# Spreading the conditioning rows over two branches, and moving merge additions and four early low parts from GpSimd to VectorE

## The chip, the core and the metric

The kernel runs on one core of a Trainium2 chip. The metric is the device time of one execution in microseconds (us). Three executions of the kernel before took 1597.98, 1598.51 and 1600.79 us (median 1598.51).

## The reference

Two layers of a hybrid backbone act on 256 latent tokens and 256 context tokens of width 1024. Both layers share this form; layer 1 needs only the latent output.

```python
sh1, sc1, g1, sh2, sc2, g2 = split(silu(c) @ w_ada[l] + b_ada[l], 6)      # conditioning: 6*1024 numbers, for c and for c_ctx
h = rms_norm(x, norm1[l]) * (1 + sc1) + sh1                               # latent; the same for the context
u_f, dn_qkv, dn_z, dn_ab, da_q, da_k, da_v, gates = split_columns(h @ w_in)
y_f  = fourier_mix(u_f) @ w_f                                             # branch F
q, k, v = silu(centred_depthwise_conv(dn_qkv))                            # 5 taps
y_dn = deltanet_output(bidirectional_deltanet(q, k, v, ...), dn_z) @ w_dn # branch D
y_da = diff_output(differential_attention(...)) @ w_da                    # branch A
g_f, g_dn, g_da = split(sigmoid(gates), 3)
y = (g_f * y_f + g_dn * y_dn + g_da * y_da) @ w_o
x = x + g1 * y
h2 = rms_norm(x, norm2[l]) * (1 + sc2) + sh2
x = x + g2 * (relu(h2 @ w_mlp1)**2 @ w_mlp2)
```

All inputs are fp32. After layer 1 a last RMSNorm gives the output.

## The kernel before

**Matmuls.** Features lie on the 128 partitions, tokens on the free axis (512 in layer 0, 256 for latent-only products). Each fp32 operand is split into a high part (rounded to fp32r) and a low part (the rest), and each product is three fp32r matmuls: high by high, low weight by high, high weight by low (`mm3`). Weights come in tiles `raw` of 128x1024 (512 KB), loaded by SyncE's DMA queue (SP) into a ring of four buffers (`raw_tile`, L238). ScalarE writes the high part `whi` (L254), and the engine `eng`, by default VectorE, writes the low part `wlo = raw - whi` (L255). Layer 1's convolution weights alternate between GpSimd and VectorE, by `turn_dn` in `load_w`. One gate chunk takes 24 matmuls, one half projection chunk 12.

**Conditioning rows.** `Rows` computes adaLN numbers as dot products on VectorE: a row tile of `w_ada` (128x1024, also in the ring `raw`) is multiplied with the silu of `c` and of `c_ctx`, with accumulation: two VectorE instructions into `junk` for one row (L336). The 24 rows 16 to 39 of layer 0 are worked off in its branches D and A: after each of the eight steps of a branch `side()` pops a number from the list `TAKE` and takes so many rows.

**Branches.** `branch(cg, cp, Y, put, side, ahead)` works through eight output chunks j: it opens the gate of a chunk `ahead` steps early (`open_gate`: 24 matmuls into a PSUM bank `pg`, then tanh on ScalarE into `gt`), multiplies Y by the projection chunk (12 matmuls into `pg`), gates the product on VectorE (`gt`, L894), and hands it to `put`. For branch F `put` spills it to DRAM; for D and A it adds it to the tile `merged` (L1148), in D on GpSimd (G), in A on VectorE (V). There are two banks `pg`, and four buffers `gt`. Branch D has three gates opened ahead (`EARLY`), so that its last three steps have no gate of their own.

**Convolution of the DeltaNet.** `dn_pair(0)` computes q, k and v of two heads: product, four multiply-adds on VectorE (`cy`, L632), tanh, `q` or `cy` (L637), then TensorE transposes them (L166). Between its products it opens four early gates of branch F; their low parts are written by GpSimd. In layer 0 the gates 0 and 1 have been produced before by `front0`, so that only gates 2 and 3 load weights there; in layer 1 all four do.

**Order.** Program order gives priorities. A scheduler that works with its own model of durations places the instructions of each engine from these; in chains such as the DeltaNet's they are given by due times (`weave`). Each engine then works through its own list in that order, and a wait holds up all that stands behind it on that engine.

Of the kernel before, what the change touches and what calls it, by code (L numbers as in the profile page):

```python
# [16 lines left out]
ALU = mybir.AluOpType  # L17
# [22 lines left out]

EARLY = 3

TAKE = [2] * 11 + [1, 1, 0, 0, 0]


NP = 3
# [8 lines left out]
C_DN, C_U, C_DA, C_Z, C_GF, C_PF, C_GA, C_PA, C_GD, C_PD, C_WO, C_M1, C_M2 = (  # L55
    0, 12, 16, 28, 32, 40, 44, 52, 56, 64, 68, 76, 108)
# [69 lines left out]
def bcast(ap, n):  # L126
    return ap.unsqueeze(2).broadcast_to([ap.shape[0], ap.shape[1], n])
# [54 lines left out]
def body(tc, A, dbg=None):  # L182
    nc = tc.nc
    weave = Weave(tc)
    V, S, G, PE = nc.vector, nc.scalar, nc.gpsimd, weave
# [47 lines left out]
    def cbank():  # L233
        return bank("pc")
# [141 lines left out]
    def rsqrt_small(x, pool, nm, bufs=2):  # L376

        w = x.shape[1]
        y, e, p_ = (pool.tile([P, 16], F32, tag=nm + c, name=nm + c, bufs=bufs)[:, :w] for c in "yep")
        S.activation(y, x.bitcast(I32), AF.Exp, scale=-0.5 * LN2 / 2 ** 23, bias=rbias)  # L380
        V.tensor_tensor(out=e, in0=y, in1=y, op=ALU.mult)
        V.tensor_tensor(out=e, in0=e, in1=x, op=ALU.mult)
        V.tensor_scalar(out=e, in0=e, scalar1=-1.0, scalar2=1.0, op0=ALU.mult, op1=ALU.add)
        V.tensor_scalar(out=p_, in0=e, scalar1=0.31282382, scalar2=0.37521049, op0=ALU.mult, op1=ALU.add)
        V.tensor_tensor(out=p_, in0=p_, in1=e, op=ALU.mult)
        V.scalar_tensor_tensor(out=p_, in0=p_, scalar=0.5, in1=e, op0=ALU.add, op1=ALU.mult)
        V.scalar_tensor_tensor(out=y, in0=p_, scalar=1.0, in1=y, op0=ALU.add, op1=ALU.mult)
        return y
# [18 lines left out]
    def square_sums(src, acc, pool, tag="sj"):  # L407

        for i in range(src.shape[1]):
            j = pool.tile([P, P], F16, tag=tag, name=tag)  # L410
            S.activation(j, src[:, i], AF.Square, accum_out=acc[:, i:i + 1])
# [54 lines left out]
    def mixer(l, last, front):  # L466
# [101 lines left out]
        def dn_pair(p):  # L568

            q2 = dp.tile([P, 2, n], F32, tag="q2", name="q2")  # L570
            k2 = dp.tile([P, 2, T], F32, tag="k2", name="k2")
            ktm = dp.tile([P, 4, 2, P], F32, tag="ktm", name="ktm")
            vtm = dp.tile([P, 4, 2, P], F32, tag="vtm", name="vtm")
            due, now, started = [], [0.0], []

            def flush(t, least=-1):

                while due and (due[0][0] <= t or min(x_[1] for x_ in due) <= least):
                    now[0], i, fn = due.pop(0)
                    with weave.chain() as at:  # L580
                        at(now[0])
                        fn()

            def later(dt, fn):
                due.append((weave.time + dt, len(started), fn))
                due.sort(key=lambda x_: x_[0])

            def finish(hh_, h, kind, m, dst):
                pt = cbank()
                for t in range(m // P):  # L590
                    PE.transpose(pt[:, t * P:(t + 1) * P], dst[:, t * P:(t + 1) * P], ident)
                pt3 = pt.rearrange("p (t c) -> p t c", c=P)[:, :m // P]
                if kind == 0:
                    square_sums(pt3, ssq[:, h], mp)
                elif kind == 1:
                    ssk = mp.tile([P, 4], F32, tag="ssk", name="ssk", bufs=2)
                    square_sums(pt3, ssk, mp)
                    V.tensor_scalar(out=ssk, in0=ssk, scalar1=EPS, scalar2=None, op0=ALU.add)
                    rk = rsqrt_small(ssk, mp, "rk")
                    V.tensor_tensor(out=ktm[:, :, hh_], in0=pt3, in1=bcast(rk, P), op=ALU.mult)  # L600
                    due.append((now[0] + POST[1], math.inf, partial(back, hh_)))
                    due.sort(key=lambda x_: x_[0])
                else:
                    S.copy(vtm[:, :, hh_], pt3)

            def back(hh_):
                pb = cbank()
                for t in range(4):
                    PE.transpose(pb[:, t * P:(t + 1) * P], ktm[:, t, hh_], ident)
                S.copy(k2[:, hh_], pb)  # L610

            for hh_ in range(2):
                h = 2 * p + hh_
                for kind in range(3):
                    f = 4 * kind + h
                    m = n if kind == 0 else T
                    ps = product(("dn", h, kind), C_DN + f, m)
                    ns = m // L
                    if p == 0 and hh_ == 1 and kind < 2:
                        for i in (2 * kind, 2 * kind + 1):  # L620
                            early[C_GF, i] = open_gate(C_GF, i, G)
                    u = dp.tile([P, 2, L + 4], F32, tag="R", name="cu", bufs=1 + last)
                    G.memset(u[:, :, 0:2], 0.0)
                    G.memset(u[:, :, L + 2:L + 4], 0.0)
                    S.copy(u[:, 0:ns, 2:L + 2], ps[:, :m].rearrange("p (s t) -> p s t", t=L))
                    started.append(f)
                    flush(weave.time, len(started) - 2)
                    y = dp.tile([P, T], F32, tag="vs", name="cy", bufs=cbuf)
                    y3 = y.rearrange("p (s t) -> p s t", t=L)[:, 0:ns]
                    S.activation(y3, ps[:, :m].rearrange("p (s t) -> p s t", t=L), AF.Copy, scale=conv[:, f, 2:3])  # L630
                    for j in (0, 1, 3, 4):
                        V.scalar_tensor_tensor(out=y3, in0=u[:, 0:ns, j:j + L], scalar=conv[:, f, j:j + 1], in1=y3,  # L632
                                               op0=ALU.mult, op1=ALU.add)
                    th = dp.tile([P, T], F32, tag="vn", name="cth", bufs=1 + last)
                    S.activation(th[:, :m], y[:, :m], AF.Tanh)
                    dst = q2[:, hh_] if kind == 0 else y
                    V.scalar_tensor_tensor(out=dst[:, :m], in0=th[:, :m], scalar=1.0, in1=y[:, :m], op0=ALU.add, op1=ALU.mult)  # L637
                    later(POST[0], partial(finish, hh_, h, kind, m, dst))
                    flush(weave.time)
            show(f"dnk{l}{p}", k2)  # L640
            show(f"dnv{l}{p}", vtm)

            def chain(lat):
                flush(math.inf)
                dn_chain(p, q2, k2, ktm, vtm, now[0] + POST[1], lat)

            return chain
# [225 lines left out]
        early = {}  # L873

        def open_gate(cg, i, eng=V):
            ps = product((cg, i), cg + i, n, eng)
            th = mp.tile([P, n], F32, tag="gt", name="gt", bufs=4)
            S.activation(th, ps[:, :n], AF.Tanh, scale=0.5)  # L878
            return th

        def branch(cg, cp, Y, put, side, ahead=2):

            ths, wpj = {i: early.pop((cg, i)) for i in range(KT) if (cg, i) in early}, None
            for i in range(KT + ahead):
                if i < KT and i not in ths:
                    ths[i] = open_gate(cg, i)
                j = i - ahead
                if j < 0:
                    continue
                if j % 2 == 0:  # L890
                    wpj = load_w(l, cp + j // 2)
                th = ths.pop(j)
                pp_ = gemm(wpj, Y, n, k0=4 * (j % 2), kts=4)
                V.scalar_tensor_tensor(out=th, in0=th, scalar=1.0, in1=pp_[:, :n], op0=ALU.add, op1=ALU.mult)  # L894
                put(j, th)
                side()
# [181 lines left out]
        yb = [yp.tile([P, 4, n], F32R, name=t_) for t_ in ("yh", "yl")]  # L1078
# [7 lines left out]
        if l == 0:  # L1086
            take = [0] * 8 + TAKE

        def side():
            k = take.pop(0)  # L1090
            if k:
                aw.step(k)
# [29 lines left out]
        for h in range(HEADS):  # L1122
            ps = gemm(load_w(l, C_Z + h), H, n)
            th = at_[0].tile([P, n], F32, tag=("zs", "zs", "q", "km")[h], name="zs", bufs=2)
# [7 lines left out]
        yd = [tp.tile([P, 4, n], F32R, name=t_) for t_ in ("ydh", "ydl")]  # L1132
# [8 lines left out]
        M = tp.tile([P, KT, n], F32, name="merged")  # L1141
# [2 lines left out]
        if l == 0:  # L1144
            aw = Rows([(0, i, 2) for i in range(16, 40)], cond_rows(tp), tp)

        def merge(eng):
            return lambda j, th: eng.tensor_tensor(out=M[:, j], in0=M[:, j], in1=th, op=ALU.add)  # L1148

        branch(C_GD, C_PD, yd, merge(G), side, 3)  # L1150
        branch(C_GA, C_PA, yb, merge(V), side)
        ax.close()
        pa_banks(f"pb{l}", 2)
        show(f"merged{l}", M)
# [358 lines left out]
```

## Time and profile before

| quantity | value |
|---|---|
| median of three executions | 1598.51 us (1597.98 to 1600.79) |
| the profiled execution's own time | 1601.47 us |
| its span, first to last instruction | 1599.7 us |
| busy share of TensorE (PE) / VectorE (DVE) / ScalarE (ACT) / GpSimd (POOL) | 95% / 73% / 46% / 12% |
| mean granted clock of TensorE | 0.989 of full speed |

The profile is one execution with times in us from the span's start. PE is matmul, PEld the weight load beside it. An idle time in brackets, as [2.98 <-DVE gt L894], is that of the engine just before the instruction, and the instruction that ended it. Branch D of layer 0 lies at about 467 to 516 us, branch A at 517 to 588, the convolution of `dn_pair(0)` at about 80 to 130 us in layer 0 and 1019 to 1070 in layer 1, branch D of layer 1 at 1324 to 1349.

### The profile page before, as it was taken

The numbers are of one execution on the slowest core, as the hardware profiler recorded it, in microseconds if no ns is written. First come the engines' busy times: TensorE is split into PE (matmuls) and PEld (weight loads), VectorE is DVE, ScalarE is ACT, GpSimd is POOL, SyncE is SP. The second block draws the span as 40 slices with busy tenths as digits, with TensorE's granted clock in tenths as the row PEclk, the third lists the DMA queues.
The fourth block names the chain that finished last, engine by engine and source line by source line (L and its number), as shares of the span: only waits on it lengthen the run. The fifth ranks groups of instructions, "written<-read, shape, count | busy, mean of one in ns | idle before, by whom it ended". The sixth has DMA issues, their size and how long they took to land.

```text
span 1599.7 us, 26147 instructions
## 1 busy us (share of the span) xinstructions
PE 1520.1 (95%) x10114; PEld 1307.5 (82%) x10114; DVE 1175.1 (73%) x2224; ACT 735.9 (46%) x1527; POOL 187.1 (12%) x195
## 2 busy tenths in 40 slices
PE   5889999999999999999999999799999999999997
PEld 2578888777887788788888888778988898999997
DVE  8687774768799777867667664876777886876765
ACT  3466543676541233423232233465547644555543
POOL 3410100011003003000000004201111102000001
PEclk9999999999999999999999999899999999999998
DMA  7522123211256654566556552141332136656662
GB/s 237 188 92 71 34 73 112 93 42 39 79 186 209 223 168 135 154 195 191 188 187 192 182 159 81 60 146 51 96 104 78 41 95 183 187 176 193 185 184 93
DMA packets 64461, 215.31 MB, mean 135 GB/s; under 512 B 7281, under 2 KB 12305, under 8 KB 64081
## 3 DMA queue, kind: packets, MB, share of 16 engines
q1 hardware_dynamic: 58178, 201.96, 40.5%
q10 hardware_dynamic: 5184, 7.21, 1.4%
q0 software_dynamic: 976, 4.48, 1.0%
q8 instruction: 79, 1.29, 0.3%
q14 instruction: 44, 0.36, 0.1%
HBM read 209.42 MB, written 4.20 MB: 134 GB/s over the span
## 4 chain that ended last, share of the span: by engine, by line
PE 69%; DVE 18%; ACT 5%; issue 4%; DMA 3%; POOL 0%; DVEq 0%; ACTq 0%; POOLq 0%
PE pg L158 35%; PE pd L158 13%; PE pa L158 11%; PE pc L158 10%; DVE junk L336 3%; DVE wlo L255 3%; DVE cy L632 3%; DMA raw<-in_wt 2%; ACT whi L254 1%; DVE mt L458 1%; ACT sw L995 1%; PE pa L166 1%; PE pc L166 1%; DMA rows<-in_rows 0%; DMA wv<-in_wt 0%
## 5 line engine op out<-in xcount | busy, mean ns | idle before, releaser
L254 ACT CAST whi<-raw 128x1024 fp32r<-128x1024 f32 x277 | 290.2, 1050 | 234.4 <-PE pg L158 93.4
L255 DVE TENSOR_TENSOR wlo<-raw,whi 128x1024 fp32r<-128x1024 f32 x263 | 327.4, 1245 | 90.4 <-ACT whi L254 87.7
L158 PE MATMUL pg<-hh,whi 128*128 128x512 f32 (+1 forms) x856 | 304.1, 355 | 0.9 <-DVE gt L894 0.7
L158 PE MATMUL pg<-hl,whi 128*128 128x512 f32 (+1 forms) x856 | 303.3, 354 | 0.0
L158 PE MATMUL pg<-hh,wlo 128*128 128x512 f32 (+1 forms) x856 | 302.7, 354 | 0.6 <-DVE wlo L255 0.6
L336 DVE CUSTOM_DVE_ANT_0 junk<-raw,cb 128x1024 f16<-128x1024 f32 x128 | 160.5, 1254 | 47.1 <-DMA raw<-in_wt 45.5
L158 PEld LDWEIGHTS pg<-hh,whi 128*128 128x128 f32 x856 | 162.7, 190 | 21.6 <-issue 1.8
L158 PEld LDWEIGHTS pg<-hl,whi 128*128 128x128 f32 x856 | 163.0, 190 | 19.3 <-issue 0.8
L158 PEld LDWEIGHTS pg<-hh,wlo 128*128 128x128 f32 x856 | 162.6, 190 | 19.0 <-DVE wlo L255 0.7
L158 PE MATMUL pg<-a,whi 128*128 128x256 f32 (+1 forms) x448 | 107.9, 325 | 0.1
L435 POOL TENSOR_TENSOR acc<-acc,sq 128x256 f32<-128x256 f32 x36 | 38.1, 1067 | 594.2 <-ACT sq L433 594.2
L632 DVE SCALAR_TENSOR_TENSOR cy<-cu,conv,cy 128x512 f32<-128x512 f32 (+1 forms) x96 | 75.4, 785 | 31.1 <-ACT cy L630 29.5
L158 PEld LDWEIGHTS pg<-a,whi 128*128 128x128 f32 x448 | 76.4, 190 | 7.9 <-DVE a L276 1.0
L158 PE MATMUL pg<-a,wlo 128*128 128x256 f32 (+1 forms) x224 | 72.4, 323 | 0.0
L878 ACT ACTIVATE gt<-pg 128x256 f32<-128x256 f32 (+1 forms) x43 | 21.0, 488 | 99.1 <-PE pg L158 82.2
L158 PE MATMUL pd<-a,whi 128*128 128x512 f32 (+1 forms) x224 | 56.7, 334 | 0.1
L158 PE MATMUL pa<-hh,whi 128*128 128x512 f32 (+1 forms) x152 | 54.2, 357 | 0.1
L158 PE MATMUL pa<-hh,wlo 128*128 128x512 f32 (+1 forms) x152 | 53.9, 355 | 0.0
L158 PE MATMUL pa<-hl,whi 128*128 128x512 f32 (+1 forms) x152 | 53.8, 354 | 0.0
L1235 DVE TENSOR_TENSOR mr<-mr 128x512 f32<-128x512 f32 (+1 forms) x64 | 35.4, 555 | 22.3 <-ACT mr L1234 22.1
L158 PE MATMUL pg<-whi,hh 128*128 128x256 f32 (+1 forms) x160 | 51.0, 319 | 0.7 <-DVE q L996 0.5
L158 PE MATMUL pg<-wlo,hh 128*128 128x256 f32 (+1 forms) x160 | 50.1, 314 | 0.0
(445 smaller groups left out, 3660.7 us busy)
## 6 DMA issues: line engine op xcount, KB each, us to landing
raw<-in_wck SPq DMA_DIRECT2D x280, 512.0 KB, 3.6
raw<-in_wt SPq DMA_DIRECT2D x80, 512.0 KB, 3.6
wv<-in_wt SPq DMA_DIRECT2D x10, 512.0 KB, 4.0
wn<-in_wn SPq DMA_DIRECT2D x16, 192.0 KB, 3.5
x<-in_xin SPq DMA_DIRECT2D x4, 512.0 KB, 8.3
spill<-gt ACTq DMA_DIRECT2D x8, 256.0 KB, 4.0
cb<-crow POOLq DMA_DIRECT2D x2, 1024.0 KB, 7.8
merged<-spill ACTq DMA_DIRECT2D x8, 256.0 KB, 3.8
```

What stands on the lines that cost most here:

```text
L158: ins = self.pe.matmul(out, a, b, start=start, stop=stop)
L166: self.pe.transpose(out, a, ident)
L254: S.copy(hi, r)
L255: eng.tensor_tensor(out=lo, in0=r, in1=hi.bitcast(F32), op=ALU.subtract)
L336: V.tensor_tensor_reduce(out=junk, in0=r, in1=self.cb[:, v], scale=0.5, scalar=0.0, op0=ALU.mult, op1=ALU.add, accum_out=ada[l][:, n, v:v ...
L435: G.tensor_tensor(out=self.acc[s], in0=self.acc[s], in1=q, op=ALU.add)
L458: V.scalar_tensor_tensor(out=t, in0=x[s][:, k], scalar=gain, in1=r[s], op0=ALU.mult, op1=ALU.mult)
L632: V.scalar_tensor_tensor(out=y3, in0=u[:, 0:ns, j:j + L], scalar=conv[:, f, j:j + 1], in1=y3, op0=ALU.mult, op1=ALU.add)
L878: S.activation(th, ps[:, :n], AF.Tanh, scale=0.5)
L995: S.copy(sw[b:b + 32], ps[b ^ 32:(b ^ 32) + 32, 0:L])
L1235: V.tensor_tensor(out=t, in0=t, in1=t, op=ALU.mult)
```

## The change

`TAKE` gets eight pairs 2, 1: 12 rows in branch D and 12 in branch A, instead of 16 and 8. In both layers the additions of branch D to `merged` go to VectorE, as those of branch A do. The low parts of the early gates that `dn_pair(0)` opens go to VectorE.

```diff
-TAKE = [2] * 11 + [1, 1, 0, 0, 0]
+TAKE = [2, 1] * 8
...
                     if p == 0 and hh_ == 1 and kind < 2:
                         for i in (2 * kind, 2 * kind + 1):
-                            early[C_GF, i] = open_gate(C_GF, i, G)
+                            early[C_GF, i] = open_gate(C_GF, i)
...
-        def merge(eng):
-            return lambda j, th: eng.tensor_tensor(out=M[:, j], in0=M[:, j], in1=th, op=ALU.add)
-
-        branch(C_GD, C_PD, yd, merge(G), side, 3)
-        branch(C_GA, C_PA, yb, merge(V), side)
+        def merge(j, th):
+            V.tensor_tensor(out=M[:, j], in0=M[:, j], in1=th, op=ALU.add)
+
+        branch(C_GD, C_PD, yd, merge, side, 3)
+        branch(C_GA, C_PA, yb, merge, side)
```

The lists of the engines move with it. First VectorE's at the end of branch D in layer 0, from the gated product of step 4 (the first `gt`) on, before; `junk` with `ada` is half a conditioning row:

```order
L894 SCALAR_TENSOR_TENSOR gt<-gt,pg 128x512
L336 ISA junk,ada_90<-raw,cb 128x1024
L336 ISA ada_90 128x1
L336 ISA junk,ada_90<-raw,cb 128x1024
L336 ISA ada_90 128x1
L894 SCALAR_TENSOR_TENSOR gt<-gt,pg 128x512
L336 ISA junk,ada_90<-raw,cb 128x1024
L336 ISA ada_90 128x1
L255 TENSOR_TENSOR wlo<-raw,whi 128x1024
L894 SCALAR_TENSOR_TENSOR gt<-gt,pg 128x512
```

The same place in the changed kernel, again from the gated product of step 4:

```order
L894 SCALAR_TENSOR_TENSOR gt<-gt,pg 128x512
L336 ISA junk,ada_90<-raw,cb 128x1024
L336 ISA ada_90 128x1
L1148 TENSOR_TENSOR merged<-merged,gt 128x512
L255 TENSOR_TENSOR wlo<-raw,whi 128x1024
L894 SCALAR_TENSOR_TENSOR gt<-gt,pg 128x512
L255 TENSOR_TENSOR wlo<-raw,whi 128x1024
L1148 TENSOR_TENSOR merged<-merged,gt 128x512
L894 SCALAR_TENSOR_TENSOR gt<-gt,pg 128x512
```

Between steps 4 and 6 stand one half row instead of three, two additions to `merged`, and two low parts instead of one. The next piece is VectorE's list in the convolution of layer 1 (`cy`, the taps, and `ge`, the decay gates), with what is new there (+) and what stood there before (-):

```order
 L520 TENSOR_SCALAR ge_9741<-gy 128x32
+L255 TENSOR_TENSOR wlo<-raw,whi 128x1024
 L521 TENSOR_TENSOR ge_9741<-ge_9741,gy 128x32
+L632 SCALAR_TENSOR_TENSOR cy<-cu,conv,cy 128x256
+L632 SCALAR_TENSOR_TENSOR cy<-cu,conv,cy 128x512
 L524 TENSOR_SCALAR ge_9741<-ge_9742 128x32
+L632 SCALAR_TENSOR_TENSOR cy<-cu,conv,cy 128x256
 L525 RECIPROCAL ge_9741<-ge_9741 128x32
+L632 SCALAR_TENSOR_TENSOR cy<-cu,conv,cy 128x256
 L526 TENSOR_TENSOR ge_9741<-ge_9741,ge_9742 128x32
```

The low part of an early gate now stands in VectorE's list, and the taps of the convolution come earlier among the gate arithmetic. Last, GpSimd's list at the same place (`Tm`, `Um` belong to the DeltaNet, the memsets to the convolution's padding):

```order
 L736 COPY Tm<-id_97 128x1024
 L737 COPY Um<-id_97 128x1024
-L255 TENSOR_TENSOR wlo<-raw,whi 128x1024 x4
+L255 TENSOR_TENSOR wlo<-raw,whi 128x1024
 L623 MEMSET cu 128x2x2
 L624 MEMSET cu 128x2x2
```

Three of the four low parts in a row have left GpSimd here; a fourth leaves it a few rows later. The convolution's own alternate weights stay.

## Rows read from the trace of the kernel before

**Rows 1.** The page, part 1: engines' busy us, share and instructions.

```profile
PE 1520.1 (95%) x10114; PEld 1307.5 (82%) x10114; DVE 1175.1 (73%) x2224; ACT 735.9 (46%) x1527; POOL 187.1 (12%) x195
```

**Rows 2.** Waits of PE, whole span: us in total, times, longest.

```profile
PE pc L166 <- DVE q L637: 9.0, 2, 6.2
PE pg L158 <- DVE gt L894: 8.2, 5, 3.0
PE pc L166 <- DVE cy L637: 5.0, 4, 2.0
```

**Rows 3.** Stages: length, busy us of each engine, PEclk, DMA share, GB/s.

```profile
85.00:100.00 15.00, 10.60 (x50) 8.26 (x49) 13.18 (x37) 8.33 (x28) 4.23 (x7) 1.00 0.31 100
505.00:520.00 15.00, 11.35 (x42) 8.59 (x41) 14.90 (x20) 3.16 (x3) 7.61 (x4) 0.89 0.68 206
520.00:575.00 55.00, 51.37 (x226) 41.88 (x225) 40.16 (x57) 14.44 (x19) 1.75 (x2) 1.00 0.62 203
1025.00:1050.00 25.00, 16.75 (x101) 14.64 (x100) 24.32 (x51) 15.01 (x42) 10.49 (x12) 0.86 0.33 96
1340.00:1350.00 10.00, 9.12 (x78) 8.74 (x77) 6.49 (x10) 3.42 (x4) 5.50 (x5) 1.00 0.72 199
```

**Rows 4.** VectorE's groups at 440 to 521 us: busy us, mean ns, idle.

```profile
L336 DVE CUSTOM_DVE_ANT_0 junk<-raw,cb 128x1024 f16<-128x1024 f32 x32 | 42.5, 1327 | 1.6 <-DMA raw<-in_wt 1.0
L255 DVE TENSOR_TENSOR wlo<-raw,whi 128x1024 fp32r<-128x1024 f32 x13 | 20.2, 1556 | 0.7 <-ACT whi L254 0.7
```

**Rows 5.** VectorE's groups at 521 to 575 us.

```profile
L336 DVE CUSTOM_DVE_ANT_0 junk<-raw,cb 128x1024 f16<-128x1024 f32 x16 | 19.6, 1224 | 9.2 <-DMA raw<-in_wt 8.9
L1148 DVE TENSOR_TENSOR merged<-merged,gt 128x512 f32<-128x512 f32 x5 | 3.4, 689 | 0.1
L894 DVE SCALAR_TENSOR_TENSOR gt<-gt,pg 128x512 f32<-128x512 f32 x5 | 3.4, 684 | 0.9 <-PE pg L158 0.9
```

**Rows 6.** Chain of waits, layer 0's output product: start, us, what.

```profile
592.09 5.44 PE pg L158 x24
```

**Rows 7.** Timeline of VectorE, branches D and A: start, us, instruction.

```profile
486.87 1.22 DVE L255 TENSOR_TENSOR wlo<-raw,whi 128x1024 fp32r<-128x1024 f32 x1
500.93 2.32 DVE L255 TENSOR_TENSOR wlo<-raw,whi 128x1024 fp32r<-128x1024 f32 x1
542.68 1.23 DVE L336 CUSTOM_DVE_ANT_0 junk<-raw,cb 128x1024 f16<-128x1024 f32 x1 [2.21 <-DMA raw<-in_wt]
```

**Rows 8.** Timeline of GpSimd, branch D.

```profile
499.94 2.21 POOL L1148 TENSOR_TENSOR merged<-merged,gt 128x512 f32<-128x512 f32 x1 [6.71 <-DVE gt L894]
```

**Rows 9.** Timeline of PE, branches D and A.

```profile
508.84 0.59 PE L158 MATMUL pg<-ydh,whi 128*128 128x512 f32 x1 [2.98 <-DVE gt L894]
512.59 0.39 PE L158 MATMUL pg<-ydh,whi 128*128 128x512 f32 x1
544.57 0.50 PE L158 MATMUL pg<-yh,whi 128*128 128x512 f32 x1 [2.98 <-DVE gt L894]
```

**Rows 10.** Timeline of VectorE, convolution of layer 1.

```profile
1021.81 2.38 DVE L516 TENSOR_SCALAR beta<-beta 128x32 f32<-128x32 f32 x1
1032.00 0.18 DVE L530 SCALAR_TENSOR_TENSOR ge<-ge,ge 128x32 f32<-128x32 f32 x1
1032.87 0.47 DVE L632 SCALAR_TENSOR_TENSOR cy<-cu,conv,cy 128x256 f32<-128x256 f32 x1
1042.02 3.81 DVE L632 SCALAR_TENSOR_TENSOR cy<-cu,conv,cy 128x256 f32<-128x256 f32 x3
```

**Rows 11.** Timeline of PE, convolution of layer 1.

```profile
1034.60 0.69 PE L166 MATMUL pc<-kc,q 128*128 128x128 f32 x2 [6.25 <-DVE q L637]
1038.36 0.60 PE L166 MATMUL pc<-kc,cy 128*128 128x128 f32 x4
```

**Rows 12.** Timeline of VectorE, convolution of layer 0.

```profile
84.24 2.31 DVE L632 SCALAR_TENSOR_TENSOR cy<-cu,conv,cy 128x512 f32<-128x512 f32 x1
86.64 0.74 DVE L632 SCALAR_TENSOR_TENSOR cy<-cu,conv,cy 128x512 f32<-128x512 f32 x1
94.02 2.38 DVE L527 TENSOR_TENSOR ge<-ge 128x32 f32<-128x32 f32 x1
```

**Rows 13.** Waits at 1290 to 1400 us, branch D of layer 1.

```profile
ACT gt L878 <- POOL merged L1148: 7.2, 3, 2.4
PE pg L158 <- DVE gt L894: 0.9, 1, 0.9
```

## The prediction

> **What bounds the kernel now.** I read the page first: TensorE (PE) is busy 95% of the span [rows 1]. The execution is a row of matmuls with gaps, and only a gap can be won or lost, since the change adds and removes no matmul. Next the waits of PE over the whole span [rows 2]. Three of the larger ones are waits for VectorE: 9.0 us for the convolution's q, 8.2 us for the gated product `gt` that frees a bank `pg`, 5.0 us for the convolution's `cy`. Third, the stages where these lie [rows 3]. PE is idle 15 - 10.60 = 4.4 us in the convolution of layer 0, 3.65 us at the end of branch D of layer 0, 3.63 us in branch A, 8.25 us in the convolution of layer 1 and 0.9 us in branch D of layer 1. In two of these five VectorE is busy 97 to 99%: 14.90 of 15 us at the end of branch D, 24.32 of 25 us in layer 1's convolution. So there the question is what VectorE must do, and how fast it does it.
>
> Its durations are not always its own. In branch D half a row takes 1327 ns and a low part 1556 ns on the mean [rows 4]; in branch A half a row takes 1224 ns [rows 5], and a low part by itself 1.22 us [rows 7]. The low part at 500.93 us that takes 2.32 us begins while GpSimd's addition of 499.94 to 502.15 us runs [rows 7, 8]: it ends 1.1 us late. So branch D's stretch costs VectorE 32 x 0.103 + 13 x 0.336 = 7.7 us beside GpSimd's eight additions, about 1 us for each. In the convolutions a full stop shows: a 32-column operation takes 2.38 us where its like takes 0.18, and three taps 3.81 us where one takes 0.47 [rows 10, 12].
>
> For this clash the Trainium skill has a rule (SBUF — State Buffer, Who interferes with whom): the port pair that VectorE and GpSimd share is an exclusive lock, and an instruction of VectorE with two SBUF inputs meets a GpSimd one that reads SBUF there; the later one stops altogether. The trace agrees, with the 2.38 us just named. Against the change stands the advice of the same skill (Perfetto Trace Analysis, Optimizing Scalar/DVE Operations) that a saturated VectorE may be relieved by giving work to others, even GpSimd, with the reservation that these two share a port. The stretched rows here bear out the reservation; what the plain advice would make of the time is the third rival.
>
> **Branch D of layer 0.** Prices: half a row 1.22, a low part 1.22, `gt` and an addition 0.69 each [rows 5, 7]; 24 matmuls take 5.44 us [rows 6], so a gate 5.44 and a half projection 2.72. Two steps with gates cost PE 16.3 us. VectorE had 8 half rows 9.8, three low parts 3.7, two `gt` 1.4, and two stretches 2.0: 16.9 us, more than PE. Now it has 6 half rows 7.3, 3.7, 1.4, and two additions 1.4: 13.8. The last three steps, without gates of their own, together with the three gates of branch A that follow cost PE 24.5 us. VectorE had 12 half rows 14.6, three `gt` 2.1, four low parts 4.9, three stretches 3: 24.6. Now 8 half rows 9.8, 2.1, three additions 2.1, 4.9: 18.9. So VectorE is no longer the bound there. What goes is the idle 3.65 us, and what follows it: after the gap of 2.98 us nine matmuls, 508.84 to 512.59 us, take 3.75 us instead of 9 x 0.227 = 2.04 [rows 9], since the granted clock fell (mean 0.89 over these 15 us, rows 3). That is 1.7 us, together 5.35. Following the new list by these prices from the first `gt` on, I find one low part late, that of the last projection chunk, by 0.4 us. I take 4.9, with the ends 0 and 5.4. The added `merged` stands behind `gt` on VectorE, and delays half rows and low parts by 0.69; PE waits for none of these within two banks' time.
>
> **Branch A of layer 0.** Its eight steps cost PE 65.3 us. VectorE now has 24 half rows 29.3, 16 `gt` and additions 11.0, 12 low parts 14.6: 55 us. It has room, but it also waits for row loads: 9.2 us before 16 half rows [rows 5], 1.15 us for a row. For 12 rows that makes 13.8, and 69 us in all, 3.5 over PE, about what is lost now (3.63). The present loss of 2.98 us [rows 9] came where two rows per step were asked for three steps long, behind a half row that waited 2.21 us for its load [rows 7]. Three steps now ask for 4 or 5 rows instead of 6: VectorE's 24.3 us (14.6 + 4.1 + 5.5) in 24.5 become at most 21.8, which leaves 2.7 for one such wait. I take 1.5 us won, with the ends -6 (two more gaps of 2.98) and +3.6. The splits of `merged` after the branch have the last row ahead of them in the list, and so do not wait for rows.
>
> **Convolution of layer 1.** Four low parts leave GpSimd. They stopped VectorE four times, the first for 2.38 - 0.18 = 2.2 us, the last for 3.81 - 3 x 0.47 = 2.4 [rows 10], 9.0 us together. On VectorE they cost 4 x 1.22 = 4.9. VectorE, 97% busy [rows 3], is through 4.1 us sooner. More comes from the order: taps stand earlier among the gate arithmetic, q follows seven taps (four at 0.47, three at 0.74), and from 1021.8 us on, with a low part before them, it is ready at about 1028.5 us, or at 1030.7 if the convolution's own low part, which stays on GpSimd, stops VectorE for 2.2 us before it; now it is waited for until 1034.60 [rows 11]. Behind that wait of 6.25 us come matmuls at half pace up to about 1038.36 [rows 11]: 3.8 us, of which half, 1.9, goes if the clock holds. The next thing late is the low part of the second early gate, which VectorE now writes behind `cy`: I price that at 1.4 us, and the wait for the `cy` before it at about 2. All idle time and the slow pace together are 8.25 + 1.9 = 10.1. I take 6.0, with the ends 0 and 10.1.
>
> **Convolution of layer 0.** Two low parts: GpSimd's stopped VectorE for 2.31 - 0.74 = 1.6 and 2.38 - 0.18 = 2.2 us [rows 10, 12], 3.8; on VectorE they cost 2.4. Here too q comes ahead of other small work in the new list. PE idles 4.4 us [rows 3]. I take 2.5, between -2.4 (both low parts in front of what PE waits for, and nothing gained) and 4.4.
>
> **Branch D of layer 1.** Three tanh wait 7.2 us for GpSimd's additions to free a buffer `gt`, and PE 0.9 us for a `gt` [rows 13]. Eight additions of half the size on VectorE, which is busy 6.49 of 10 us there [rows 3], are hidden. I take 0.6, between 0 and 0.9.
>
> **Sum.** 4.9 + 1.5 + 6.0 + 2.5 + 0.6 = 15.5 us. The profiled execution took 1601.5 us, 3.0 above the median of the three runs; so 1586 on its scale, and 1598.5 - 15.5 = 1583 on theirs. Both ends together: -8.4 and +24.4, that is 1607 to 1574.
>
> **Rivals.** *The low parts only change their queue.* VectorE is freed in branch D, but in the convolutions PE now waits for low parts written late on VectorE. For it: VectorE's list there has no idle time. Against it: 9.0 us of stops against 4.9 of work. Branches alone give 4.9 + 0.6, and 1593 us. *The gap moves on.* What branch D wins branch A loses, as rows come where there were none, and the convolutions win 2 to 3 us by half: 1597, no change by what can be told (0.2%, 3.2 us). *A saturated VectorE gets more work.* If GpSimd's work cost VectorE nothing, the convolutions would lose 4.9 + 2.4 and branch D win its 4.9: 1601, within or just over 0.2%. The stretches in rows 4, 10 and 12 speak against it. *Branch A waits for its rows.* The slow side: VectorE takes things in order, and each row load that is late holds up the next `gt`. Room in branch A is 65.3 - 55 = 10.3 us, and with the present loss of 3.6 and the other gains of 14.0, 27.9 us in all; from 2.3 us per row for 12 rows the kernel is slower. At 2.98 each VectorE needs 90.8 us: 25.5 lost instead of 3.6, and 1598.5 - 14.0 + 21.9 = 1606. Single rows do wait 2.21 us [rows 7], but the mean is 1.15.
>
> **How the numbers follow.** The forecast gets 0.66 (own range 1577 to 1591), the first rival 0.17, the gap that moves 0.08, the saturated VectorE 0.04, branch A's rows 0.05. Faster by over 0.2% are the forecast and most of the first rival (0.16), and a little of the second (0.02): 0.84. Slower are the last and a part of the third: 0.06. The range that holds eight in ten goes from 1575 to 1596.
>
> **What would show it.** In the changed kernel's profile no `merged` on GpSimd; half rows in branch D at about 1.22 us and low parts near 1.22; no wait of PE for `gt` near the end of branch D, and the granted clock at 1.0 there; in layer 1's convolution the wait for q down from 6.25 us to under 2.5, no 32-column operation over 2 us but one; VectorE's waits for row loads in branch A at about 14 us, with no gap of PE over 3 us behind them. I am wrong if PE's waits in the convolutions keep their sum under other names, or if branch A shows several gaps.

## The result, and the profile after

The changed kernel takes 1583.64 us (median of four executions, 1582.70 to 1584.71), the kernel before, timed beside it, 1598.24; the ratio is 0.9911, with a 95% interval of 0.9893 to 0.9929. The forecast was 1583. Its total came out; several of its terms did not.

The page's first part (busy us and share of each engine) and the waits of PE over the whole span stand against [rows 1, 2]:

```profile
PE 1517.0 (96%) x10114; PEld 1305.2 (82%) x10114; DVE 1166.3 (74%) x2246; ACT 735.4 (46%) x1527; POOL 145.0 (9%) x173
```

```profile
PE pc L166 <- DVE cy L637: 5.8, 3, 3.6
PE pg L158 <- DVE gt L894: 0.9, 1, 0.9
PE pc L166 <- DVE q L637: 0.3, 1, 0.3
```

VectorE does 22 instructions more and is busy 8.8 us less; GpSimd loses 42.1 us. PE's waits for `gt` fall from 8.2 to 0.9 us, those for `q` from 9.0 to 0.3. Those for `cy` grow, from 5.0 to 5.8. The stages, in the order of [rows 3], each at its new place (length, busy us of PE, PEld, DVE, ACT, POOL, granted clock, DMA share, GB/s):

```profile
85.00:100.00 15.00, 15.00 (x73) 12.16 (x72) 14.72 (x43) 11.00 (x34) 0.73 (x7) 1.00 0.28 79
501.00:516.00 15.00, 15.00 (x67) 12.39 (x67) 13.84 (x21) 3.65 (x4) 0.53 (x1) 1.00 0.82 256
516.00:571.00 55.00, 54.13 (x239) 44.53 (x238) 45.17 (x68) 16.93 (x22) 0.00 (x0) 1.00 0.61 193
1011.00:1036.00 25.00, 20.14 (x130) 17.98 (x129) 20.54 (x57) 16.94 (x47) 3.31 (x9) 0.86 0.36 108
1323.00:1333.00 10.00, 9.84 (x84) 9.44 (x84) 8.78 (x15) 3.60 (x5) 0.00 (x0) 1.00 0.66 201
```

At the first two places PE is now never idle, and in branch D the clock no longer falls. In layer 1's convolution 4.86 us of idle time stay, and the clock is as low as before (0.86).

To see where time was won, take landmarks that both traces have, and the length of the stretch between two of them. This frees each stage from what came before it. The landmarks are the start of DVE L507 and of DVE L786 (first and last work of a convolution), of the first `ydh` and the last `ydl` matmul (branch D), and of the last `gt` of branch A. Each column is one profiled execution, in us; the four middle ones are experiments below.

| stretch | before | rows only | additions only | low parts only | rows and additions | after |
|---|---|---|---|---|---|---|
| convolution, layer 0 | 45.77 | 45.73 | 45.70 | 40.73 | 45.70 | 40.70 |
| branch D, layer 0 | 48.59 | 48.06 | 43.41 | 48.55 | 43.47 | 43.50 |
| branch A, layer 0 | 71.22 | 71.80 | 72.39 | 69.76 | 68.84 | 68.84 |
| A to the convolution of layer 1 | 432.65 | 430.18 | 433.19 | 429.74 | 428.01 | 430.79 |
| convolution, layer 1 | 53.98 | 53.77 | 53.93 | 51.22 | 53.76 | 50.61 |
| granted clock in the fourth stretch (1.00 is full speed) | 0.98 | 0.99 | 0.98 | 1.00 | 1.00 | 0.99 |

Where nothing in them was edited, the two convolutions and branch D repeat within 0.3 us in this table. Branch A differs by 1.5 us (before, low parts only), and the fourth stretch by 5 us, among kernels that were not edited there. The fourth stretch is the longer the lower TensorE's granted clock was in it (last row of the table). So the 1.9 us won there by the changed kernel can't be put down to the change. The profiled executions scatter: their spans differ by 17.1 us while the medians differ by 14.6.

VectorE's groups in the stretch with branch D (436 to 517 us), and then in branch A (516 to 571 us), answer to [rows 4, 5] (busy us, mean ns, idle before):

```profile
L336 DVE CUSTOM_DVE_ANT_0 junk<-raw,cb 128x1024 f16<-128x1024 f32 x28 | 34.2, 1221 | 4.2 <-DMA raw<-in_wt 3.9
L255 DVE TENSOR_TENSOR wlo<-raw,whi 128x1024 fp32r<-128x1024 f32 x15 | 18.3, 1219 | 0.8 <-ACT whi L254 0.8
```

```profile
L336 DVE CUSTOM_DVE_ANT_0 junk<-raw,cb 128x1024 f16<-128x1024 f32 x20 | 24.5, 1223 | 10.0 <-DMA raw<-in_wt 9.6
```

Half a row takes 1221 ns instead of 1327, a low part 1219 instead of 1556: the stretches are gone. In branch A VectorE is idle 10.0 us before these 20 half rows, 9.6 of it for their loads. Over the whole branch it is 10.9 us before 24 half rows, where 13.8 were expected.

In layer 1's convolution, where `q` was waited for 6.25 us [rows 11], stands now (PE, VectorE, GpSimd: start, duration, [idle before]):

```profile
1014.78 0.44 PE L166 MATMUL pc<-kc,q 128*128 128x128 f32 x2 [0.33 <-DVE q L637]
1019.22 1.12 PE L166 MATMUL pc<-kc,cy 128*128 128x128 f32 x4 [3.65 <-DVE cy L637]
```

```profile
1016.23 2.33 DVE L530 SCALAR_TENSOR_TENSOR ge<-ge,ge 128x32 f32<-128x32 f32 x1
1018.49 0.68 DVE L637 SCALAR_TENSOR_TENSOR cy<-cth,cy 128x512 f32<-128x512 f32 x1
```

```profile
1015.75 2.77 POOL L255 TENSOR_TENSOR wlo<-raw,whi 128x1024 fp32r<-128x1024 f32 x1
```

The wait for `q` is gone. A new one of 3.65 us, for `cy`, has come. In front of that `cy` a 32-column operation that takes 0.18 us elsewhere takes 2.33, and it ends when GpSimd's low part ends (1018.56 and 1018.52). This is a low part of the convolution's own alternate weights, which the change left on GpSimd.

### The profile page after: what moved, and what is told of

It reads as the page before. It is cut to its first block, busy times and chain, and to the rows that moved or that the text cites. A ratio compares the mean times of both kernels' runs of the same rounds, so it can differ in the third digit from the quotient of the medians.

```text
span 1582.6 us, 26109 instructions
## 1 busy us (share of the span) xinstructions
PE 1517.0 (96%) x10114; PEld 1305.2 (82%) x10114; DVE 1166.3 (74%) x2246; ACT 735.4 (46%) x1527; POOL 145.0 (9%) x173
## 5 line engine op out<-in xcount | busy, mean ns | idle before, releaser
L336 DVE CUSTOM_DVE_ANT_0 junk<-raw,cb 128x1024 f16<-128x1024 f32 x128 | 157.0, 1227 | 57.8 <-DMA raw<-in_wt 56.3
L632 DVE SCALAR_TENSOR_TENSOR cy<-cu,conv,cy 128x512 f32<-128x512 f32 (+1 forms) x96 | 69.3, 723 | 30.3 <-ACT cy L630 29.0
L1235 DVE TENSOR_TENSOR mr<-mr 128x512 f32<-128x512 f32 (+1 forms) x64 | 35.4, 555 | 23.6 <-ACT mr L1234 23.6
```

What stands on the lines that cost most here:

```text
L336: V.tensor_tensor_reduce(out=junk, in0=r, in1=self.cb[:, v], scale=0.5, scalar=0.0, op0=ALU.mult, op1=ALU.add, accum_out=ada[l][:, n, v:v ...
L1235: V.tensor_tensor(out=t, in0=t, in1=t, op=ALU.mult)
```

## The experiments

Each was timed in five rounds beside the kernel before. Ratios are to that kernel.

**1. The rows alone.**

```diff
-TAKE = [2] * 11 + [1, 1, 0, 0, 0]
+TAKE = [2, 1] * 8
```

> Only the list of conditioning rows is changed (12 + 12 instead of 16 + 8); additions and low parts stay on GpSimd. My theory (GpSimd's instructions stop VectorE's, and rows and additions both load VectorE in branch D): VectorE gets four half rows less in the last three steps of branch D, 4.9 us, which covers the gap of 3.65 us and the slow matmuls behind it, while the eight stretches of about 1 us stay; branch A wins or loses up to 2 us. 1592 to 1596 beside 1598 for the kernel before. Rival 1, the rows explain branches D and A fully (the additions on VectorE give nothing): about 1590.5, that is the 7.5 us that the two branches won. Rival 2, moved work only costs VectorE: this kernel reaches the changed kernel's 1583.6 or less.

1598.45 us, ratio 1.0004 (0.9993 to 1.0016): nothing. All three expectations fail, mine too. PE's gap at the end of branch D is still there, and VectorE's list ahead of the `gt` that ends it shows why:

```profile
508.26 0.60 PE L158 MATMUL pg<-ydh,whi 128*128 128x512 f32 x1 [2.68 <-DVE gt L894]
```

```profile
499.20 1.22 DVE L255 TENSOR_TENSOR wlo<-raw,whi 128x1024 fp32r<-128x1024 f32 x1
500.34 2.32 DVE L336 CUSTOM_DVE_ANT_0 junk<-raw,cb 128x1024 f16<-128x1024 f32 x1
...
506.39 1.22 DVE L255 TENSOR_TENSOR wlo<-raw,whi 128x1024 fp32r<-128x1024 f32 x1
507.53 0.68 DVE L894 SCALAR_TENSOR_TENSOR gt<-gt,pg 128x512 f32<-128x512 f32 x1
```

From the `gt` before (498.61) to this one stand four half rows, one of them stretched to 2.32 us beside GpSimd's addition, and two low parts: 8.9 us, as before the change (499.18 to 508.10). The list put a low part where a half row had gone. The sum over the last three steps had room; the step in front of the gap had not. In branch A VectorE waits 13.6 us for row loads:

```profile
L336 DVE CUSTOM_DVE_ANT_0 junk<-raw,cb 128x1024 f16<-128x1024 f32 x21 | 25.7, 1223 | 13.9 <-DMA raw<-in_wt 13.6
```

**2. The additions alone.**

```diff
-        branch(C_GD, C_PD, yd, merge(G), side, 3)
+        branch(C_GD, C_PD, yd, merge(V), side, 3)
```

> Only branch D's additions go to VectorE, in both layers. My theory: eight stretches of about 1 us (7.7 us) go from VectorE's time in branch D of layer 0, eight additions of 0.69 (5.5) come; 2.2 us of VectorE's time are won, of the 3.65 us gap some 2 go, with a little of the slow pace behind it, and 0.5 us in branch D of layer 1: 1594.5 to 1596.5 beside 1598. Rival 1, the stretches cost nothing that counts: 1598 or, with 5.5 us more work on a saturated VectorE, 1600 to 1603. Rival 2, the additions alone take the gap away: 1592.

1595.07 us, ratio 0.9988 (0.9974 to 1.0001), at the edge of what can be told. The theory's range holds it, but by another way. In the trace, of an execution of 1601.21 us, branch D wins 5.2 us, all that it wins in the changed kernel; so Rival 2 is right on the place. But some of it is lost at once where branch A begins (PE, then ScalarE):

```profile
513.87 0.50 PE L158 MATMUL pg<-hh,whi 128*128 128x512 f32 x1 [1.88 <-ACT whi L254]
516.65 0.65 PE L158 MATMUL pg<-hh,wlo 128*128 128x512 f32 x1 [2.28 <-DVE wlo L255]
```

```profile
509.83 1.05 ACT L254 CAST whi<-raw 128x1024 fp32r<-128x1024 f32 x1 [8.30 <-DMA raw<-in_wck]
```

The weights of the next gates come late: ScalarE waits 8.30 us for a tile of the ring that weights and rows share. With VectorE out of the way, the ring, which carries 16 rows in branch D, limits the start of branch A. Experiment 5 tests this.

**3. The low parts alone.**

```diff
-                            early[C_GF, i] = open_gate(C_GF, i, G)
+                            early[C_GF, i] = open_gate(C_GF, i)
```

> Only the low parts of the early gates go to VectorE, two in layer 0 and four in layer 1. My theory: the stretch of the convolutions wins what the comparison of the traces shows there, 5.1 us in layer 0 and 3.4 in layer 1, and the branches nothing: 1589 to 1591 beside 1598. Rival 1, the low parts only change their queue: 1597 to 1600. Rival 2, the 1.9 us won between branch A of layer 0 and the convolution of layer 1 also hang on these low parts, by the order of the lists: 1587 to 1588.

1590.49 us, ratio 0.9957 (0.9942 to 0.9972). The theory's range holds it; "the low parts only change their queue" is refuted. The convolution of layer 0 wins 5.0 us, that of layer 1 2.8. PE's waits for `gt` stay, and that for `cy` is the changed kernel's:

```profile
PE pg L158 <- DVE gt L894: 6.7, 5, 3.0
PE pc L166 <- DVE cy L637: 5.8, 3, 3.6
```

**4. All of layer 1's low parts on VectorE.** The changed kernel, and in `load_w`:

```diff
-            eng = (G, V)[turn_dn[0] % 2]
+            eng = V
```

> The changed kernel, and in it the convolution's own alternate weights of layer 1 get their low parts on VectorE too, so that GpSimd writes none there. My theory: in layer 1 TensorE waits 3.65 us for cy since one such low part on GpSimd stopped VectorE for 2.2 us ahead of it; without it that wait goes down by about 2 us and the slow pace behind it by 1: 1580 to 1582.5 beside 1583.6 for the changed kernel. Rival 1, VectorE is at its bound there and each of these low parts costs it 1.22 us: 1585 to 1589. Rival 2, their place is off the critical path: 1583 to 1584.

1575.63 us, ratio 0.986 (0.984 to 0.9879), 8.0 us under the changed kernel's median: more than I expected, and against both rivals. At the place of the new wait (PE, VectorE):

```profile
1012.61 1.11 PE L166 MATMUL pc<-kc,cy 128*128 128x128 f32 x4 [1.85 <-DVE cy L637]
```

```profile
1011.77 0.19 DVE L530 SCALAR_TENSOR_TENSOR ge<-ge,ge 128x32 f32<-128x32 f32 x1
1011.87 0.69 DVE L637 SCALAR_TENSOR_TENSOR cy<-cth,cy 128x512 f32<-128x512 f32 x1
```

The 2.33 us operation takes 0.19, the wait is halved, and the convolution takes 48.83 us instead of 50.61. More low parts of this kind stood elsewhere in layer 1. Here is one at its start, in the changed kernel on GpSimd, and what VectorE does beside it; then the same products of the norm (`mt`) in this experiment:

```profile
984.43 2.52 POOL L255 TENSOR_TENSOR wlo<-raw,whi 128x1024 fp32r<-128x1024 f32 x1
```

```profile
983.88 3.36 DVE L458 SCALAR_TENSOR_TENSOR mt<-x1l,ma,r 128x256 f32<-128x256 f32 x2
```

```profile
983.28 1.65 DVE L458 SCALAR_TENSOR_TENSOR mt<-x1l,ma,r 128x256 f32<-128x256 f32 x3
```

Two `mt` in 3.36 us become three in 1.65. What that is worth shows in PE's waits for `nd` and `hl` of this norm, in the changed kernel and then in this experiment:

```profile
977.76 0.49 PE L158 MATMUL pd<-kc,nd 128*128 128x128 f32 x2 [2.07 <-DVE nd L402]
988.09 0.40 PE L158 MATMUL pc<-hl,wab 128*16 128x256 f32 x1 [2.13 <-DVE hl L461]
```

```profile
977.57 0.60 PE L158 MATMUL pd<-kc,nd 128*128 128x128 f32 x3 [0.58 <-DVE nd L402]
```

All seven traces without this edit have these waits of 2.07 and 2.13 us. Here the second is gone and the first is 0.58, with 0.36 more for `nd` later. PE's waits for `cy` fall from 5.8 to 2.2 us in the whole span. Together these are 6.9 of the 8.0 us.

**5. The changed kernel with the old rows.**

```diff
-TAKE = [2, 1] * 8
+TAKE = [2] * 11 + [1, 1, 0, 0, 0]
```

> The changed kernel with the old list of rows (16 in branch D, 8 in branch A): additions and low parts are on VectorE. The single parts gave: rows nothing (ratio 1.0004), additions 0.9988, low parts 0.9957, together 0.9949, while the whole change gave 0.9911. Theory: rows and additions need each other. With 16 rows in branch D the ring of weight tiles is late there once VectorE is not (the run with the additions alone shows TensorE waiting 1.88 us for whi, 2.28 for wlo, behind loads that are 8.3 us late): here 1588 to 1590.5, ratio about 0.9945. Rival: the parts simply add up, and the single runs were measured too low: then this kernel lies at the changed kernel's 1584 plus nothing, 1583 to 1585.

1587.5 us, ratio 0.9931 (0.9914 to 0.9947): 0.5 us under the theory's range, above the rival's, and 3.9 us over the changed kernel's median, which was timed in other rounds. Branch D takes 43.41 us in the trace, branch A 72.16 instead of 68.84: the rows are worth 3.3 us, all of it in branch A. PE waits there for the same two weights as in experiment 2:

```profile
508.76 0.49 PE L158 MATMUL pg<-hh,whi 128*128 128x512 f32 x1 [1.79 <-ACT whi L254]
511.62 0.79 PE L158 MATMUL pg<-hh,wlo 128*128 128x512 f32 x1 [2.37 <-DVE wlo L255]
```

In the changed kernel, which differs by the rows alone, neither wait is left.

**6. Rows and additions without the low parts.**

```diff
-                            early[C_GF, i] = open_gate(C_GF, i)
+                            early[C_GF, i] = open_gate(C_GF, i, G)
```

> The changed kernel with the low parts of the early gates on GpSimd again: the new list of rows and branch D's additions on VectorE. Theory (rows and additions need each other): about the 7.1 us that the traces of before and after differ by between the start of branch D and the end of branch A: 1590 to 1592, ratio 0.995 to 0.9965, although the two parts alone gave 1.0004 and 0.9988. Rival (the parts add up): 0.9992, about 1596.5.

1593.07 us, 1.1 us over the theory's range in time, and ratio 0.996 (0.9948 to 0.9973), inside its range in ratio, while the two parts alone gave 1.0004 and 0.9988. They need each other: the interval leaves the rival's 0.9992 out. Branches D and A take 43.47 and 68.84 us, as in the changed kernel, and the end of branch D reads as there:

```profile
505.00:520.00 15.00, 15.00 (x68) 12.43 (x67) 14.21 (x21) 3.65 (x4) 0.53 (x1) 1.00 0.82 250
```

The last six go on from experiment 4, to see how far the rule carries.

**7. The front's low parts too.** In the front of layer 0 five `load_w(..., G)` lose their `G`:

```diff
-job(("dn", 0, 0), load_w(0, C_DN, None, G), "pg")
+job(("dn", 0, 0), load_w(0, C_DN, None), "pg")
...
```

> The kernel with all of layer 1's low parts on VectorE (1575.63 us), and in it also the five low parts that GpSimd writes at the start of layer 0 (three convolution weights, two gates). My theory (a low part costs VectorE 1.22 us itself and 2.2 us when GpSimd writes it beside a two-input instruction of VectorE): up to 5 x 1 us at the start, where VectorE is busy 8 tenths: 1571 to 1575.5. Rival: VectorE is the bound in the first 60 us and what it gets there costs the full 5 x 1.22 = 6.1 us: 1579 to 1582.

1569.2 us, ratio 0.9814 (0.9798 to 0.9831): the theory's direction, 1.8 us below its range. At the start of the kernel PE waits for a sum of squares, in the changed kernel 11.12 us. PE's row, and VectorE's and GpSimd's ahead of it there:

```profile
25.42 0.80 PE L158 MATMUL pg<-oneD,tot 128*128 128x1 f32 x3 [11.12 <-DVE tot L1276]
```

```profile
17.98 2.55 DVE L1276 TENSOR_TENSOR tot<-sq 128x256 f32<-128x256 f32 x1
20.46 2.82 DVE L1276 TENSOR_TENSOR sq<-sq 128x512 f32<-128x512 f32 x1
```

```profile
16.82 5.92 POOL L255 TENSOR_TENSOR wlo<-raw,whi 128x1024 fp32r<-128x1024 f32 x2 [2.15 <-ACT whi L254]
```

And in the experiment (VectorE, PE):

```profile
17.84 0.41 DVE L1276 TENSOR_TENSOR tot<-sq 128x256 f32<-128x256 f32 x1
18.18 0.68 DVE L1276 TENSOR_TENSOR sq<-sq 128x512 f32<-128x512 f32 x1
```

```profile
21.00 1.01 PE L158 MATMUL pg<-oneD,tot 128*128 128x1 f32 x4 [6.84 <-DVE tot L1276]
```

The wait falls by 4.3 us, since these two instructions take 0.41 and 0.68 us instead of 2.55 and 2.82.

**8. The norms' additions too, without 7.**

```diff
-                G.tensor_tensor(out=self.acc[s], in0=self.acc[s], in1=q, op=ALU.add)
+                V.tensor_tensor(out=self.acc[s], in0=self.acc[s], in1=q, op=ALU.add)
```

> The kernel with all of layer 1's low parts on VectorE (1575.63 us), and in it also the 36 additions of squares for the norms (acc, 128x256, 1084 ns each on GpSimd). My theory: they lie in the output products, where VectorE has room; each costs VectorE 0.4 us, and frees it of stops where the norm's small operations and hl follow; the wait of TensorE for nd (3.4 us in total) goes down by 1 to 2 us: 1573 to 1575.5. Rival 1: nothing on the critical path changes: 1575 to 1576.5. Rival 2: the additions delay the products that empty TensorE's banks: 1577 to 1581.

1570.36 us, ratio 0.9822 (0.9806 to 0.9838), less than any of the expectations. But see the next.

**9. Experiments 7 and 8 together.**

> The low parts of the front (ratio 0.9814 with all of layer 1's) and the norms' additions (0.9822) on VectorE together, on the kernel with all of layer 1's low parts there (0.986). Theory (separate places, GpSimd's stops there go each for itself): the gains add, 0.9814 + 0.9822 - 0.986 = 0.9776, 1561 to 1565 us. Rival (the second only shifts work onto a VectorE that is now the bound): 0.9805 to 0.983, 1567 to 1571.

1568.89 us, ratio 0.9809 (0.9792 to 0.9825). Beside experiment 7 (0.9814) the norms' additions give nothing that can be told; the gains do not add to 0.9776. The rival's number is right. That VectorE became the bound is not shown, and why experiment 8 was faster than 4 stays open.

**10. The low parts of layer 0's norm too.** On top of 9:

```diff
-                modulate(0, xv, r_, ma, 0, s, k, st, G)
+                modulate(0, xv, r_, ma, 0, s, k, st)
```

> As the kernel with the front's low parts and the norms' additions on VectorE, and in it also the 16 low parts hl of layer 0's first norm, 128x256, that GpSimd subtracts at 35 to 75 us (VectorE computes them with one instruction from mt, the shift and hh, and ScalarE's second pass over mt goes). Theory: TensorE's waits for hl (1.8 us) and the stops go; 16 x 0.47 = 7.5 us more for VectorE, which is busy 7 to 8 tenths there: 1 to 3 us less than that kernel. Rival: VectorE is the bound while the first convolution starts, and the 7.5 us delay its taps: 1 to 4 us more.

1563.71 us, ratio 0.9773 (0.9758 to 0.9789), the lowest median of all, 35.4 us under the kernel before (1599.13 in these rounds). The theory had the direction, but 5.2 us under experiment 9 is more than its 1 to 3. The trace doesn't show the gain at its place: from the start to the first convolution it leads experiment 9 by 0.2 us only.

**11. The additions of the identity to C too.** On top of 10, `G` becomes `V` at L726:

```diff
-                    G.tensor_tensor(out=part(C32, i), in0=part(C32, i),
+                    V.tensor_tensor(out=part(C32, i), in0=part(C32, i),
```

> As the kernel with hl on VectorE, and in it also the 16 additions of the identity to C (128x512, 1427 ns each on GpSimd) in the DeltaNet's chains, 0.68 each on VectorE. Theory: each addition on GpSimd stops VectorE for up to 1.4 us in a chain where TensorE waits 2.2 us for C; with 16 x 0.7 = 11 us of work for 10 to 15 us of stops nothing or up to 3 us are won. Rival: the additions stand in VectorE's list between steps of the chain that have nothing to do with them, and cost up to 16 x 0.68 = 11 us: 3 to 11 us more.

1571.39 us, ratio 0.9827 (0.9811 to 0.9843): slower than 10 by 7.7 us, as the rival said. VectorE's additions, and a wait of PE that was 0.6 us in experiment 10:

```profile
L726 DVE TENSOR_TENSOR C<-C,kc 128x512 f32<-128x512 f32 x16 | 11.0, 687 | 2.7 <-ACT C L725 2.6
PE pd L158 <- DVE X L745: 2.8, 5, 0.8
```

VectorE stands 2.7 us for ScalarE's `C` before these additions, and PE then waits for `X`, which comes behind them. These rows show 2.2 us of the 7.7.

**12. The rotary products too.** On top of 11, `G` becomes `V` at L999:

```diff
-                G.tensor_tensor(out=sw, in0=sw, in1=sin, op=ALU.mult)
+                V.tensor_tensor(out=sw, in0=sw, in1=sin, op=ALU.mult)
```

> As the one before, and in it also the 16 products sw of the rotary embedding (128x256, 794 ns on GpSimd, 0.41 on VectorE): no instruction with two inputs in SBUF is left on GpSimd, only copies, casts, fills and DMA issues. Theory (every such instruction on GpSimd costs VectorE more than it would cost there): no slower than the one before, 0 to 1.5 us less. Rival (it pays only where VectorE has two-input work at that moment): 0 to 3 us more.

1564.46 us, ratio 0.978 (0.9765 to 0.9796), 6.9 us faster than 11 and level with 10: the direction is the theory's, the size far beyond it. PE's wait for `X` is 0.9 us here. In the traces 4.5 of the 6.9 us lie between the end of layer 1's convolution and the end of its branch D (273.0 us in 11, 268.6 here, 270.3 in 10). Whether 12 took back what 11 had lost, by another order of instructions, or won it by its own edit stays open: the kernel with 12's products and without 11's additions was not tried.

## Why the forecast was right in sum and wrong in parts

*VectorE's stretches.* Right. With the additions gone from GpSimd every half row and low part in branch D has its own 1.22 us. The third rival (a saturated VectorE gets more work) falls: each of experiments 2, 3, 4 and 7 gave VectorE more instructions, and none was slower. The Trainium skill's rule (SBUF — State Buffer, Who interferes with whom), that the later of the two stops until the other has ended, is met to 0.04 us by the 2.33 us operation above. The advice of the Trainium skill (Perfetto Trace Analysis, Optimizing Scalar/DVE Operations) that work may be given away from a busy VectorE finds at most one case here, experiment 11. But the prediction told the stop as one of instructions with two SBUF inputs, and one of its two rows of 2.38 us, `beta` at 1021.81 [rows 10], is a TENSOR_SCALAR with one input. The stop reaches further than that; the last section has a second case.

*Branch D of layer 0.* 4.9 predicted, 5.1 measured. The size held, but the working gave it to rows and additions together. The additions alone bring 5.2, the rows alone 0.5. By the prediction's own prices this could have been seen: 24.6 us less three stretches, plus three additions, is 23.7, already under PE's 24.5.

*Branch A of layer 0.* 1.5 predicted, 2.4 measured. The step that failed is the reason: the rows were to ease `TAKE`'s bursts, and alone they win nothing there (71.80). They pay once the additions have moved. Then VectorE no longer holds branch D back, the weights of branch A's first gates come late, and four rows fewer in the ring pay 3.3 us with the low parts on VectorE (72.16 to 68.84) and 3.55 without (72.39 to 68.84). The prediction asked what is late next on VectorE, and did not ask it of the ring. The slow rival, branch A waiting for its rows, did not come: 10.9 us of idle time of VectorE before them, the longest gap of PE 0.87. Nor did the gap move on from branch D, as the second rival had it.

*Convolution of layer 0.* 2.5 predicted, 5.1 measured, and about 5 in every kernel with these low parts on VectorE. The term was mis-sized: it charged both low parts to a VectorE without idle time. But VectorE stood idle 1.75 us ahead of `q`, for a load of `in_rows` that GpSimd issued behind its own low part. In the trace of before (GpSimd, then VectorE):

```profile
85.94 0.58 POOL L345 DMA_DIRECT2D raw<-in_rows  x1
```

```profile
89.66 0.23 DVE L351 CUSTOM_DVE_ANT_0 raw<-raw 128x64 f32<-128x64 f32 x1 [1.75 <-DMA raw<-in_rows]
90.10 0.69 DVE L637 SCALAR_TENSOR_TENSOR q<-cth,cy 128x512 f32<-128x512 f32 x1
```

And after:

```profile
84.73 0.58 POOL L345 DMA_DIRECT2D raw<-in_rows  x1 [9.46 <-issue]
```

```profile
86.26 1.21 DVE L255 TENSOR_TENSOR wlo<-raw,whi 128x1024 fp32r<-128x1024 f32 x1
87.39 0.68 DVE L637 SCALAR_TENSOR_TENSOR q<-cth,cy 128x512 f32<-128x512 f32 x1
88.92 0.22 DVE L351 CUSTOM_DVE_ANT_0 raw<-raw 128x64 f32<-128x64 f32 x1
```

In the new list `q` stands ahead of the instruction that needs the load, so it no longer waits for it; and the load, issued 1.2 us earlier, is there when it is needed (88.92). From the stage's landmark, the first L507, to `q` VectorE takes 3.3 us instead of 6.4: gone are this wait, the stop of 1.6 us [rows 12] and about 1 us of small operations that now stand behind `q`, and one low part of 1.1 us has come. So PE's whole 4.4 us went, and the upper end, 4.4, was too low as well. What the order alone would bring was not tried.

*Convolution of layer 1.* 6.0 predicted, 3.4 measured (2.8 in experiment 3). Mis-sized the other way. `q` comes in time: ready 8.6 us after the stage's landmark, where I had worked out 8.8, or 11.0 with a stop. The wait for the next `cy`, priced at about 2, is 3.65, since the low part left on GpSimd stops VectorE right ahead of it. I had let this stop fall on `q`. Experiment 4 shows the cause by taking it away. Nor did the 1.9 us for the slow matmuls come: behind the new wait they start 0.21 us apart instead of 0.11 up to 1024.77, and the granted clock of the stage stays at 0.86. The sign I named for being wrong, PE's waits keeping their sum under other names, came in part: waits for `q` and `cy` were 14.0 us and are 6.1.

*Branch D of layer 1.* 0.6 predicted. The 0.9 us wait for `gt` [rows 13] is gone; the stretch from the first `ydh` to the last `gt` is 0.45 shorter, no more than it differs among kernels with the same edit there.

*The sum.* These stretches give 5.09 + 2.38 + 5.07 + 3.37 + 0.45 = 16.4 us by the traces, 14.6 by the medians, 15.5 by the prediction: two terms too low, one too high. That the total hit is in part luck.

## What to carry to other kernels

Before moving work off an engine that seems idle, look for instructions of VectorE that take 2 us where their like takes 0.2, and see what GpSimd does at that moment: here each move of low parts from GpSimd paid, though VectorE looked full, while the norms' additions gave nothing once the front's low parts had moved, and those to C cost time. Test the parts of such a change alone and together, since one part can hide the other's worth: the rows gave nothing until the additions had moved. After each step ask what is late next on every shared thing, the ring of loads too, not only on the engine that was freed.

## What the runs showed of the hardware

A stop does not hit large operations only: on VectorE a 128x32 `ge` took 2.33 us, a sum of 128x512 squares 2.82 instead of 0.68, a half row of the custom product 2.32 instead of 1.23, each beside one of GpSimd's subtractions or additions. Nor is it bound to two inputs: before the change a cast of 128x32 with one input took 2.35 us, where its like took 0.17. It ended at 1040.83 us, and GpSimd's low part, begun at 1038.03, at 1040.80:

```profile
1038.48 2.35 DVE L540 CAST ghr<-g 128x32 fp32r<-128x32 f32 x1
1041.90 0.17 DVE L544 CAST glr<-glo 128x32 fp32r<-128x32 f32 x1
```

GpSimd's own low parts differ too (2.52 us at 984 us, 2.77 at 1016, two in 5.92 at the start); whether VectorE held them up was not tried.
